# Reordering three stage starts and the last rows of a Griffin layer kernel

## The chip, the cores and the metric

The kernel runs on one core of one Trainium2 chip. A core has TensorE for matmuls (PE in the rows, PEld for the loading of weights, which overlaps), VectorE (DVE), ScalarE (ACT), GpSimd (POOL) and SyncE (SP). SyncE and GpSimd also issue the transfers between the chip's memory (HBM) and the on-chip memory (SBUF). The metric is the device time of one execution in microseconds (us), as a median over runs.

## The reference

One layer of a streaming encoder is computed for 2112 tokens: 2048 of a prompt and 64 of a running stream. In short:

```
h = rmsnorm(x, norm_mix) @ w_in               # split into RG-LRU, attention and gate parts
x1 = x + (lru_part * ... + attention_part) @ w_out
h = rmsnorm(x1, norm_ffn) @ w_up              # 1024 -> 2 * 2816 rows
h = causal_dwconv(h, width 3) + bias          # along time, every row by itself
h = silu(gate rows) * value rows              # 2816 rows
x2 = x1 + h @ w_down                          # 2816 -> 1024
y = rmsnorm(x2, norm_final)
```

The outputs also hold the newest keys, values and states. The change touches nothing in this arithmetic; it concerns the part from `w_up` on.

## The kernel before

**Precision.** Each float32 operand is split into a high part `hi` (a copy in a rounded type, on ScalarE, L205) and a low part `lo = src - hi` (on VectorE, L206); a product is three matmuls, hi·hi, hi·lo and lo·hi. A matmul thus waits for a ScalarE copy and then for a VectorE subtraction. `put2` and `split2` make the copy and hand back the subtraction, to be placed later; three lists hold such subtractions: `plow` (up-projection weights), `dlow` (down-projection operands) and the local list of the token code.

**Tokens.** The 2112 tokens form three pairs of blocks: 304 and 304, 304 and 304, 448 and 448. A pair's tokens of the first and the second block and the halves of the weights form a 2 × 2 block product, done with seven products and sums ahead of and behind them. The products' names in order are 11, T3, T2, T4, T1, 21, 22.

**Up-projection** (profile lines 1066 to 1240, and the loop at 1425). `plan` lists the steps. A step is one product `u` (0 to 6) for two "lanes" of 128 gate or value rows: 24 matmuls (L1105 to L1107). For the first two pairs the two lanes are the two pairs, and weights are read and combined anew (loads L951, combinations L983, stored for later with L971); 22 times 7 steps. Then the third pair follows, 11 times 7 steps, whose lanes are a gate row and a value row block, with the weights stored before (read at L979) and with token operands read back by `xread` (L1050). Behind product u=3, VectorE makes the value rows' first half in a tile G (L1154), behind u=4 the second half (L1156), behind u=5 the gate rows' first half (L1161); ScalarE handles u=0, 1, 2 (L1150) and u=6 (L1163). A PSUM bank is shared by products 0, 2, 4 and 6, so u=6 writes where L1156 reads. Then come the convolution (its first tap on ScalarE, L1135; two more on VectorE for each lane, L1141, four instructions in a row), Silu (L1166), the gating (L1175, L1177), and the sums for the down-projection (L1184 to L1192), stored to `hS`.

**Around it.** `x1prep` prepares the second pair's (index 1) last three operands T1, 21 and 22 while steps 0 to 3 run: it loads the rows of x1, scales them by the norm (L852 on VectorE, L854 and L855 on GpSimd), subtracts (L865), and splits them (L206; L873 and L874 on ScalarE and GpSimd). `norms(2)` makes the third pair's norms (matmul L750, square root L751, reciprocal L752) at step 1 and stores them to `rS`, from which SyncE reads them later (L1008).

**Down-projection** (loop `for j, ... in enumerate(seq)`). `seq` lists product, pair, k (11 blocks of rows), the output row tiles and the columns; an entry is 4 row tiles × 3 matmuls (L1612 to L1614). Weights (`dweights`) and tokens (`dtoken`, read from `hS` at L1272) are split by L206. When k reaches 10, VectorE adds the PSUM results into the sums R (L1652). `drive(side, n)` advances side work by n pieces: at first the rest of the up-projection (`flushing`), later the residual (`resid`, L1564), the squares (`squares`, L1579) and the norm with the output stores (`outputs`, scaling L1592, store L1594). The last product of the first pair ends the program: first two row tiles at 304 columns, then the other two in column halves of 152, each half with its own squares, norm and stores.

**Order.** The program is scheduled by hand: an engine does its instructions in the order in which the code issues them, and only waits for others.

## Time and profile before

| | |
|---|---|
| Median of three runs | 2996.58 us (2990.6 to 2997.52) |
| Profiled run | 2998.43 us, span 2996.7 us |
| Granted TensorE clock, mean | 0.982 |
| TensorE busy | 2874.9 us (96%) |
| VectorE busy | 2059.3 us (69%) |
| ScalarE busy | 1544.9 us (52%) |
| GpSimd busy | 465.2 us (16%) |
| Up-projection | 1578 to 2514 us |
| Down-projection | 2514 to 2987 us, end at 2996.7 |

The profile is of one execution. A timeline row is start, duration, engine, line, operation, output <- input, shape, and the count of like instructions in a row; brackets give the idle time before it and what ended it. A row of the waits gives who waits <- for whom, then total us, times, and the longest. A row of a group gives busy us and mean ns, then idle us before. A window row gives its stretch and length, then for each engine busy us and count, the granted clock (1.00 is full), the DMA share and GB/s.

### The profile page before, as it was taken

To read this page: it belongs to the slowest core of one execution; us is meant where nothing else is said; L and a number is where in the kernel's file an instruction comes from. 1 tells how busy PE (TensorE), PEld (TensorE's weight loads), DVE (VectorE), ACT (ScalarE), POOL (GpSimd) and SP (SyncE) were. 2 spreads that over 40 slices of the span, in tenths; PEclk is the share of its full clock that TensorE was granted. 3 is DMA by queue.
4 is the path that set the end of the run, shared out by engine and by line. 5 is a ranking of instruction groups with operands and counts; after the bars stand their busy time and mean duration, and the time that the engine had idled before them with its cause. 6 is when DMAs were issued, how large, how long until landed. Compare 5 with 4: busy or idle time off the path is not lost. (4 is left out here: it accounts for less than half of the span.)

```text
span 2996.7 us, 48641 instructions
## 1 busy us (share of the span) xinstructions
PE 2874.9 (96%) x17640; PEld 2758.7 (92%) x17640; DVE 2059.3 (69%) x4012; ACT 1544.9 (52%) x3412; POOL 465.2 (16%) x667
## 2 busy tenths in 40 slices
PE   8989999999998999998998999999899999999998
PEld 6989889999998999997997999999799998999997
DVE  5288884277786177776568888888665656666677
ACT  4577772466763367765324555555444444433432
POOL 3232212000000000002324333323111111000011
PEclk9999999999999999999998999999999999999999
DMA  7866547644335734437875565555766666976563
GB/s 239 277 217 204 179 165 229 196 130 133 128 113 186 213 124 139 140 107 259 279 232 181 199 216 207 208 201 198 253 208 218 214 224 193 272 213 211 156 214 118
DMA packets 319185, 583.81 MB, mean 195 GB/s; under 512 B 36464, under 2 KB 221792, under 8 KB 302048
## 3 DMA queue, kind: packets, MB, share of 16 engines
q1 hardware_dynamic: 280544, 449.91, 47.5%
q0 software_dynamic: 38400, 130.79, 11.6%
q8 instruction: 139, 2.28, 0.3%
q14 instruction: 102, 0.84, 0.1%
HBM read 389.46 MB, written 191.64 MB: 194 GB/s over the span
## 5 line engine op out<-in xcount | busy, mean ns | idle before, releaser
L230 PE MATMUL mm<-xh,whl 128*128 128x320 f32 (+2 forms) x2112 | 691.3, 328 | 10.2 <-ACT xh L200 5.5
L231 PE MATMUL mm<-xl,whl 128*128 128x320 f32 (+2 forms) x2112 | 689.0, 326 | 10.2 <-DVE xl L201 5.7
L232 PE MATMUL mm<-xh,whl 128*128 128x320 f32 (+2 forms) x2112 | 687.2, 326 | 1.3 <-POOL whl L201 1.3
L205 ACT ACTIVATE RE<-FW 128x512 fp32r<-128x512 f32 (+2 forms) x540 | 289.0, 559 | 408.3 <-DVE FW L983 101.1
L206 DVE TENSOR_TENSOR RE<-FW,RE 128x512 fp32r<-128x512 f32 (+2 forms) x540 | 315.3, 604 | 173.9 <-ACT RE L205 163.7
L231 PEld LDWEIGHTS mm<-xl,whl 128*128 128x128 f32 x2112 | 402.1, 190 | 18.4 <-DVE xl L201 8.2
L230 PEld LDWEIGHTS mm<-xh,whl 128*128 128x128 f32 x2112 | 402.3, 191 | 17.8 <-ACT xh L200 8.7
L232 PEld LDWEIGHTS mm<-xh,whl 128*128 128x128 f32 x2112 | 402.1, 190 | 2.3 <-POOL whl L201 1.6
L1141 DVE SCALAR_TENSOR_TENSOR FA<-FA,pkt 128x608 f32<-128x608 f32 (+1 forms) x264 | 245.2, 950 | 65.1 <-ACT FA L1135 60.3
L1107 PE MATMUL mf<-RA,RE 128*128 128x304 f32 (+1 forms) x620 | 203.1, 328 | 3.6 <-DVE RE L206 3.6
L1105 PE MATMUL mf<-RA,RE 128*128 128x304 f32 (+1 forms) x620 | 203.3, 328 | 2.0 <-ACT FA L1150 1.7
L1613 PE MATMUL mf<-RE 128*128 128x304 f32 (+2 forms) x616 | 198.1, 322 | 6.6 <-DVE RE L206 6.6
L1106 PE MATMUL mf<-RA,RE 128*128 128x304 f32 (+1 forms) x620 | 202.6, 327 | 0.0
L1612 PE MATMUL mf<-RE 128*128 128x304 f32 (+2 forms) x616 | 198.1, 322 | 2.4 <-DVE RR L1652 2.4
L1614 PE MATMUL mf<-RE 128*128 128x304 f32 (+2 forms) x616 | 197.3, 320 | 0.0
L1106 PE MATMUL mf<-RE 128*128 128x304 f32 (+1 forms) x480 | 158.9, 331 | 15.3 <-DVE RE L206 15.3
L1105 PE MATMUL mf<-RE 128*128 128x304 f32 (+1 forms) x480 | 158.4, 330 | 4.3 <-ACT RE L205 4.3
L1135 ACT ACTIVATE FA<-FA,pkt 128x608 f32<-128x608 f32 (+1 forms) x132 | 128.1, 970 | 63.2 <-DVE FA L1156 61.0
L1107 PE MATMUL mf<-RE 128*128 128x304 f32 (+1 forms) x480 | 158.5, 330 | 0.0
L201 POOL TENSOR_TENSOR gl<-gr,gh 128x256 fp32r<-128x256 f32 x24 | 22.4, 932 | 787.9 <-ACT gh L200 787.9
L510 ACT ACTIVATE pr<-S,nm 128x256 f32<-128x256 f32 (+1 forms) x272 | 123.0, 465 | 12.6 <-DVE nm L506 12.4
L1107 PE MATMUL mm<-RE 128*128 128x304 f32 (+1 forms) x400 | 127.7, 319 | 0.0
(332 smaller groups left out, 7129.1 us busy)
## 6 DMA issues: line engine op xcount, KB each, us to landing
whl<-wiS SPq DMA_DIRECT2D x88, 1024.0 KB, 5.3
wiS<-whl SPq DMA_DIRECT2D x44, 1024.0 KB, 4.8
wuS<-RE POOLq DMA_DIRECT2D x88, 512.0 KB, 4.0
RE<-wuS SPq DMA_DIRECT2D x88, 512.0 KB, 4.3
FW<-in_w_up_dram SPq DMA_DIRECT2D x154, 256.0 KB, 4.4
hS<-FA POOLq DMA_DIRECT2D x154, 152.0 KB, 3.8
FW<-hS SPq DMA_DIRECT2D x154, 152.0 KB, 3.6
FW<-in_w_in_dram SPq DMA_DIRECT2D x44, 512.0 KB, 5.7
```

The lines of the kernel that those rows point to most:

```text
L205: nc.scalar.activation(hi, src, AF.Copy)
L206: return lambda: nc.vector.tensor_tensor(lo, src, hi.bitcast(F32), op=ALU.subtract)
L230: nc.tensor.matmul(ps[:, :n], wh[:, c], xh[:, k, :n], start=first, stop=False)
L231: nc.tensor.matmul(ps[:, :n], wh[:, c], xl[:, k, :n], start=False, stop=False)
L232: nc.tensor.matmul(ps[:, :n], wl[:, c], xh[:, k, :n], start=False, stop=last)
L1105: nc.tensor.matmul(ps[:, :n], w[:, 0, c], x[:, k, 0], start=first, stop=False, **more)
L1106: nc.tensor.matmul(ps[:, :n], w[:, 0, c], x[:, k, 1], start=False, stop=False, **more)
L1107: nc.tensor.matmul(ps[:, :n], w[:, 1, c], x[:, k, 0], start=False, stop=last, **more)
L1141: nc.vector.scalar_tensor_tensor(uc, G[:, j:j + self.cols], col("fw", 44 * j + m), uc, op0=ALU.mult, op1=ALU.add)
L1612: nc.tensor.matmul(ps[m][:, cs], w[:, 0, c], t[:, 0], start=k == 0, stop=False)
L1613: nc.tensor.matmul(ps[m][:, cs], w[:, 0, c], t[:, 1], start=False, stop=False)
L1614: nc.tensor.matmul(ps[m][:, cs], w[:, 1, c], t[:, 0], start=False, stop=k == 10)
```

## The change

1. `x1prep` takes its operands one by one from a list: T1's four pairs first, then 21 and 22. Every scaling is one fused VectorE instruction and every low part is VectorE's; GpSimd's part is gone. Eight buffers are loaded ahead, further loads follow one or two at a time. It is driven by 3, 3, 4 and 0 pieces in steps 0 to 3, the rest in step 3.
2. `norms(2)` and the store of `rS` move from step 1 to step 5.
3. For the third pair, the pool of the gate and value rows G takes its tiles from the other end of its region (`right=True`), and the pending weight low parts `plow` are issued at the start of each step's preparation, whether or not a preparation follows.
4. In the first part of the down-projection, pending low parts `dlow` are issued ahead of the side work.
5. At k = 10 the side work is driven behind the additions, not ahead of them.
6. The last two row tiles run one after the other at 304 columns, in place of two column halves.

```diff
@@ -838,42 +838,34 @@
         for o in ("T1", "21", "22"):
             operand(p, o)
         where = {"11": (0, t0), "12": (0, t1), "21": (4, t0), "22": (4, t1)}
-        x = {}
-
-        def load(k):
-            if k < 4:
-                for o, (half, t) in where.items():
-                    x[o, k] = tp.tile([P, n], F32, name="x" + o, bufs=2)
-                    nc.sync.dma_start(x[o, k], x1S[k + half, :, t:t + n])
-
-        def scale(o, k, eng):
+        todo = [(o, k) for k in range(4) for o in ("12", "11")] + [(o, k) for o in ("21", "22") for k in range(4)]
+        raw, low = [], []
+
+        def load(j):
+            if j < len(todo):
+                half, t = where[todo[j][0]]
+                raw.append(tp.tile([P, n], F32, name="x1", bufs=8))
+                nc.sync.dma_start(raw[j], x1S[todo[j][1] + half, :, t:t + n])
+
+        for j in range(8):
+            load(j)
+        yield
+        for j, (o, k) in enumerate(todo):
             half, t = where[o]
-            if eng is nc.vector:
-                eng.scalar_tensor_tensor(x[o, k], x[o, k], col("g2", k + half), rs[t], op0=ALU.mult, op1=ALU.mult)
-            else:
-                eng.tensor_scalar(x[o, k], x[o, k], col("g2", k + half), None, op0=ALU.mult)
-                eng.tensor_tensor(x[o, k], x[o, k], rs[t], op=ALU.mult)
-
-        load(0)
-        load(1)
-        yield
-        for k in range(4):
-            scale("11", k, nc.vector)
-            scale("12", k, nc.vector)
-            scale("21", k, nc.gpsimd)
-            scale("22", k, nc.vector if k % 2 else nc.gpsimd)
-            nc.vector.tensor_tensor(x["11", k], x["12", k], x["11", k], op=ALU.subtract)
-            yield
-            low = put2(p, "T1", k, x["11", k])
-            yield
-            low()
-            los = []
-            for o in ("21", "22"):
-                t = xops[p, o]
-                nc.scalar.activation(t[:, k, 0], x[o, k], AF.Copy)
-                nc.gpsimd.tensor_tensor(t[:, k, 1], x[o, k], t[:, k, 0].bitcast(F32), op=ALU.subtract)
-            yield
-            load(k + 2)
+            nc.vector.scalar_tensor_tensor(raw[j], raw[j], col("g2", k + half), rs[t], op0=ALU.mult, op1=ALU.mult)
+            while low:
+                low.pop(0)()
+                load(len(raw))
+                if j < 10:
+                    load(len(raw))
+            if o == "12":
+                continue
+            if o == "11":
+                nc.vector.tensor_tensor(raw[j], raw[j - 1], raw[j], op=ALU.subtract)
+                o = "T1"
+            low.append(put2(p, o, k, raw[j]))
+            yield
+        low.pop()()
 
     rsum = {}
     phases = [PAIRS[0], PAIRS[1], PAIRS[2]]
@@ -1277,8 +1269,7 @@
 
     seq = [(i, p, k, range(4), slice(0, PAIRS[p][0][1])) for i in range(7)
            for p in ((2, 0, 1) if i == 0 else (0, 1, 2) if i < 6 else (2, 1)) for k in range(11)]
-    seq += [(6, 0, k, r, c) for r, c in ((range(2), slice(0, BS)), (range(2, 4), slice(0, BS // 2)),
-                                         (range(2, 4), slice(BS // 2, BS))) for k in range(11)]
+    seq += [(6, 0, k, r, slice(0, BS)) for r in (range(2), range(2, 3), range(3, 4)) for k in range(11)]
 
     DRAWS = (10, 13, 16, 19, 22, 24, 26, 28, 30, 32, 34)
 
@@ -1450,7 +1441,7 @@
 
             for pool in up["c"], up["u"], up["h"]:
                 pool.close()
-            up["c"], up["u"], up["h"] = Pool(FA), Pool(FA), Pool(FP)
+            up["c"], up["u"], up["h"] = Pool(FA, right=True), Pool(FA), Pool(FP)
             up["c"].reserve("G", 2 * BM + 2, 3)
             up["u"].reserve("uc", 2 * BM + 2, 4)
         for lane in live:
@@ -1458,6 +1449,8 @@
         if last <= i < last + 7:
             give(0, u)
             give(1, u)
+        while plow:
+            plow.pop(0)()
         while made < len(plan) + 1 and fits(i):
             prepare(made)
             made += 1
@@ -1467,21 +1460,21 @@
             lane.after(u)
         rounded()
         if i < 4:
-            drive(x1, 3)
+            drive(x1, (3, 3, 4, 0)[i])
             if i == 0:
                 io[2].close()
                 wr.extend("wr", 4 * P, 2)
-            if i == 1:
-                norms(2)
-                for t0, n in PAIRS[2]:
-                    nc.gpsimd.dma_start(rS[:, t0:t0 + n], rsum[t0])
             if i == 3:
                 drive(x1, 99)
                 x1.clear()
                 tp.close()
                 sums[1].close()
-                sums[2].close()
                 up["u"].reserve("uc", 2 * BS, 4)
+        if i == 5:
+            norms(2)
+            for t0, n in PAIRS[2]:
+                nc.gpsimd.dma_start(rS[:, t0:t0 + n], rsum[t0])
+            sums[2].close()
         if i == 6:
             up["s"].close()
             up["s"], up["h"] = Pool(FW), Pool(FA, right=True)
@@ -1626,7 +1619,12 @@
                 tparts(len(seq) - 36 + k)
             if k < 6:
                 raw[6, 0, k - 2] = dtoken("T4", 0, k - 2)
-        drive(side, 5 if R is None else 1 if i < 4 else 2 if (i, p) != (6, 0) or j < len(seq) - 22 else 3)
+        pace = 5 if R is None else 1 if i < 4 else 2 if (i, p) != (6, 0) or j < len(seq) - 22 else 3
+        if R is None:
+            while dlow:
+                dlow.pop(0)()
+        if k < 10:
+            drive(side, pace)
         if j == 8:
 
             drive(side, 99)
@@ -1666,6 +1664,7 @@
                 add("11", "11")
             if i == 6:
                 add("21", "21")
+        drive(side, pace)
         if i == 2:
             side.append(resid(p, "11"))
         if i == 3:
```

In the order of VectorE's instructions, the change shows at these places. Line numbers of the changed kernel are lower by 8 around the up-projection (L1148 is L1156 of before, L1133 is L1141, L975 is L983, L864 is L865); L855 is the new scaling, in place of L852.

VectorE in the up-projection's steps 1 to 3 before, from two scalings and a subtraction of pair 1's operands on (FA holds these, FW weights and norms, RE split operands):

```order
L852 SCALAR_TENSOR_TENSOR FA<-FA,pkt,FW 128x304 x3
L865 TENSOR_TENSOR FA<-FA 128x304
L752 RECIPROCAL FW<-FW 128x448 x2
L206 TENSOR_TENSOR RE<-FW,RE 128x512
L983 TENSOR_TENSOR FW<-FW 128x512
L206 TENSOR_TENSOR RE<-FA,RE 128x304
L852 SCALAR_TENSOR_TENSOR FA<-FA,pkt,FW 128x304 x2
L865 TENSOR_TENSOR FA<-FA 128x304
L206 TENSOR_TENSOR RE<-FW,RE 128x512
L1154 TENSOR_TENSOR FA<-mf,FA 128x304
L1154 TENSOR_TENSOR FA<-mm,FA 128x304
L206 TENSOR_TENSOR RE<-FA,RE 128x304
```

VectorE in steps 3 to 5 of the changed kernel:

```order
L855 SCALAR_TENSOR_TENSOR FA<-FA,pkt,FW 128x304
L206 TENSOR_TENSOR RE<-FA,RE 128x304
L855 SCALAR_TENSOR_TENSOR FA<-FA,pkt,FW 128x304
L206 TENSOR_TENSOR RE<-FA,RE 128x304 x2
L206 TENSOR_TENSOR RE<-FW,RE 128x512
L975 TENSOR_TENSOR FW<-FW 128x512
L1148 TENSOR_TENSOR FA<-mf,FA 128x304 x2
L206 TENSOR_TENSOR RE<-FW,RE 128x512
L975 TENSOR_TENSOR FW<-FW 128x512
L1133 SCALAR_TENSOR_TENSOR FA<-FA,pkt 128x608 x4
L1153 TENSOR_TENSOR FA<-mm,FA 128x304 x2
L752 RECIPROCAL FW<-FW 128x448 x2
```

The two reciprocals L752 stood between the operands of k = 1 and k = 2, ahead of step 3's evictions L1154; they now stand behind step 5's evictions L1153, and operand by operand a scaling is followed by a low part.

VectorE at the down-projection's start before (FP and FW hold tokens and weights, RE the split parts; the 448-wide L206 are tokens):

```order
L206 TENSOR_TENSOR RE<-FW,RE 128x512 x2
L1141 SCALAR_TENSOR_TENSOR FA<-FA,pkt 128x898 x4
L206 TENSOR_TENSOR RE<-FW,RE 128x448 x4
L206 TENSOR_TENSOR RE<-FW,RE 128x512
L1175 TENSOR_TENSOR FP<-FA 128x832
L1177 TENSOR_TENSOR FP<-FA 128x64
```

The same place in the changed kernel:

```order
L206 TENSOR_TENSOR RE<-FW,RE 128x512 x2
L206 TENSOR_TENSOR RE<-FW,RE 128x448 x4
L206 TENSOR_TENSOR RE<-FW,RE 128x512
L1133 SCALAR_TENSOR_TENSOR FA<-FA,pkt 128x898 x4
L206 TENSOR_TENSOR RE<-FW,RE 128x448
L206 TENSOR_TENSOR RE<-FW,RE 128x512
```

The four token low parts and a weight's stood behind the convolution L1141 and stand ahead of it now (L1133).

VectorE at the end of the program before, from the scalings of the pair's other block on (RR holds the sums, FD the squares and norms):

```order
L1592 SCALAR_TENSOR_TENSOR RR<-RR,pkt,FD 128x304 x8
L1579 TENSOR_TENSOR FD<-FD 128x304 x2
L1652 TENSOR_TENSOR RR<-mf,RR 128x152 x2
L1579 TENSOR_TENSOR FD<-FD 128x152 x2
L752 RECIPROCAL FD<-FD 128x152
L1592 SCALAR_TENSOR_TENSOR RR<-RR,pkt,FD 128x152 x8
L1652 TENSOR_TENSOR RR<-mf,RR 128x152 x2
L1579 TENSOR_TENSOR FD<-FD 128x152 x2
L752 RECIPROCAL FD<-FD 128x152
L1592 SCALAR_TENSOR_TENSOR RR<-RR,pkt,FD 128x152 x8
```

The same place in the changed kernel (L1585 is L1592, L1572 is L1579, L1650 is L1652):

```order
L1585 SCALAR_TENSOR_TENSOR RR<-RR,pkt,FD 128x304 x8
L1572 TENSOR_TENSOR FD<-FD 128x304 x2
L1650 TENSOR_TENSOR RR<-mf,RR 128x304
L1572 TENSOR_TENSOR FD<-FD 128x304
L1650 TENSOR_TENSOR RR<-mf,RR 128x304
L1572 TENSOR_TENSOR FD<-FD 128x304
L752 RECIPROCAL FD<-FD 128x304
L1585 SCALAR_TENSOR_TENSOR RR<-RR,pkt,FD 128x304 x8
```

Two sets of additions, squares, reciprocal and eight scalings at 152 columns become one set at 304, with the row tiles' additions apart.

## The prediction

> **What bounds the kernel now.** I read the busy times first, then who TensorE (PE) waits for in the second half of the program, then the busy times stage by stage, then the timelines at the places found.
>
> ```profile
> span 2996.7 us, 48641 instructions
> PE 2874.9 (96%) x17640; PEld 2758.7 (92%) x17640; DVE 2059.3 (69%) x4012; ACT 1544.9 (52%) x3412; POOL 465.2 (16%) x667
> PE mf L1106 <- DVE RE L206: 15.3, 5, 5.2
> PE mf L1613 <- DVE RE L206: 6.6, 1, 6.6
> 1578.48:1621.18 42.70, 30.11 (x174) 27.44 (x172) 37.96 (x47) 16.00 (x37) 26.14 (x29) 0.80 0.52 179
> 2113.14:2167.07 53.93, 41.26 (x170) 36.07 (x169) 33.74 (x58) 23.14 (x53) 5.34 (x10) 0.87 0.75 262
> 2514.28:2550.95 36.67, 30.07 (x133) 26.90 (x132) 22.21 (x37) 18.44 (x39) 4.31 (x8) 0.86 0.76 234
> 1630.00:1640.00 10.00, 10.00 (x73) 10.00 (x73) 6.03 (x13) 4.43 (x11) 0.68 (x2) 1.00 0.60 205
> 2200.00:2210.00 10.00, 10.00 (x50) 9.09 (x49) 5.94 (x7) 7.22 (x20) 0.00 (x0) 1.00 0.50 157
> ```
>
> Columns of the stage rows: length, busy time of PE, of its weight loads, of VectorE (DVE), ScalarE (ACT) and GpSimd (POOL), granted clock, DMA share, GB/s. PE is the bound: 96% of the span, and 10.00 of 10 us inside a stage. There a 304-wide matmul costs 10/73 = 0.137 us and a 448-wide one 10/49 = 0.204 (by the weight loads), so a step of 24 costs 3.3 and 4.9. What the change can win lies where PE stops: three stage starts, of 42.70, 53.93 and 36.67 us, at a granted clock of 0.80 to 0.87. In all three the missing operand is a low part (L206 on VectorE). The edit touches them, the additions that close a down-projection pass, and the end.
>
> **A. Start of the up-projection (pair-1 operands, norms).**
>
> ```profile
> 1578.48 0.30 PE L1105 MATMUL mf<-RA,RE 128*128 128x304 f32 x1
> 1601.82 0.62 PE L1106 MATMUL mf<-RE 128*128 128x304 f32 x1 [4.11 <-DVE RE L206]
> 1621.18 0.30 PE L1105 MATMUL mf<-RA,RE 128*128 128x304 f32 x1
> 1584.86 1.15 DVE L852 SCALAR_TENSOR_TENSOR FA<-FA,pkt,FW 128x304 f32<-128x304 f32 x2
> 1588.79 4.12 DVE L852 SCALAR_TENSOR_TENSOR FA<-FA,pkt,FW 128x304 f32<-128x304 f32 x3
> 1594.34 5.76 DVE L752 RECIPROCAL FW<-FW 128x448 f32<-128x448 f32 x2 [1.04 <-ACT FW L751]
> 1613.07 0.85 DVE L1156 TENSOR_TENSOR FA<-mf,FA 128x304 f32<-128x304 f32 x2
> L852 DVE SCALAR_TENSOR_TENSOR FA<-FA,pkt,FW 128x304 f32<-128x304 f32 x10 | 8.5, 896 | 0.0
> L206 DVE TENSOR_TENSOR RE<-FW,RE 128x512 fp32r<-128x512 f32 x10 | 8.5, 857 | 2.5 <-ACT RE L205 2.4
> 2974.53 3.66 DVE L1592 SCALAR_TENSOR_TENSOR RR<-RR,pkt,FD 128x304 f32<-128x304 f32 x8
> 2538.07 2.36 DVE L206 TENSOR_TENSOR RE<-FW,RE 128x448 fp32r<-128x448 f32 x4
> ```
>
> Steps 0 to 6 run from 1578.48 to 1621.18; their 168 matmuls are worth 168 × 0.137 = 23.0. The difference, 19.7, less 1.5 for the norms' own matmuls, is the most that A can win: about 18. In between VectorE is busy 37.96 of 42.70, in the order the rows show: operands of pair 1, the two reciprocals of the third pair (5.76, with 1.04 of waiting ahead), more operands, and only at 1613.07 the evictions L1156 that free the bank into which step 6 writes.
>
> The edit removes GpSimd's twenty tensor instructions, and gives VectorE 16 scalings (10 before), 4 subtractions and 12 low parts (4 before): 14 more 304-wide instructions. It takes the reciprocals behind step 5's evictions. Priced as where VectorE works alone: a scaling 3.66/8 = 0.46; another 304-wide one 0.85/2 = 0.42; a 448-wide low part is 2.36/4 = 0.59, so a 512-wide one about 0.65. Ahead of the end of L1156 there now stand 16 scalings (7.3), 20 other 304-wide ones (4 subtractions, 12 low parts, 4 evictions: 8.5) and 7 of 512 (4.5), in all 20.3. From the first, at 1584.9, they end at 1605.2, where they ended at 1613.9. Each is there in time before that: T1 needs 16 instructions (some 7.9, 1592.8, with step 4 at about 1593), operand 21 twelve more.
>
> So step 6 begins at 1605.2 and step 7 at about 1608.5 to 1609, against 1621.18. What is late next is the reciprocals: they begin behind the first four L1141 and L1161, at about 1609.4, last 5.76, and two weight low parts follow, to 1616.5; step 9 needs these at 1609 + 2 × 3.3 = 1615.7 and waits 0.8. The net gain I take is **11.4**. Nothing on the DMA side moves: the same 16 loads, in 8 buffers one behind the other; the 20 ScalarE copies are the same.
>
> The unknown is the contended price. In this stage ten scalings cost 0.896 each and ten 512-wide low parts 0.857, beside a GpSimd busy for 26.14 us; alone they cost 0.46 and 0.65. At the high price throughout, 16 × 0.896 + 20 × 0.80 + 7 × 0.857 = 36.3, L1156 would end at 1621, and step 6, which began at 1621.18 − 3.3 = 1617.9, would begin 3.3 later: a loss. I take the low price because GpSimd's tensor work, the only thing on that engine that is longer than an issue, is gone. Bounds −3.3 and +14.
>
> The Trainium skill, page "SBUF — State Buffer", section "Who interferes with whom", says that a VectorE instruction with two inputs in SBUF contends with a GpSimd instruction that reads SBUF, the first one there blocking the other whole. The 4.12 us for three scalings beside 0.46 each alone look like that. By the page A is worth the 11.4; if the slow rows have another cause it is worth less, down to the lower bound.
>
> **B. Third pair's gate rows at the other end; weight low parts flushed each step.**
>
> ```profile
> 2117.36 0.47 PE L1107 MATMUL mf<-RA,RE 128*128 128x448 f32 x1 [3.65 <-DVE RE L206]
> 2149.56 0.73 PE L1106 MATMUL mf<-RE 128*128 128x448 f32 x1 [5.24 <-DVE RE L206]
> 2148.35 0.62 DVE L1154 TENSOR_TENSOR FA<-mf,FW 128x448 f32<-128x448 f32 x1 [4.67 <-DMA hS<-FA]
> 2160.89 0.74 PE L1106 MATMUL mf<-RE 128*128 128x448 f32 x1 [3.41 <-DVE RE L206]
> 2154.64 4.60 DVE L1141 SCALAR_TENSOR_TENSOR FA<-FA,pkt 128x898 f32<-128x898 f32 x4
> 2151.43 1.81 ACT L205 ACTIVATE RE<-FP 128x448 fp32r<-128x448 f32 x3 [5.08 <-DMA FP<-xS]
> RE<-wuS SPq DMA_DIRECT2D x14, 512.0 KB, 7.0
> ```
>
> The first two waits (3.65 and 5.24) go: the low parts that PE waited for at 2117.36 now stand ahead of the conv (L1141) on VectorE, and L1154 no longer waits 4.67 for a store (hS from FA) to free old rows, behind which three low parts were queued. But PE's next needs do not move with it. The kept weights of the second step are loads of 512 KB that take 7.0 here and are issued as before; a PE that is 3.65 earlier waits for them. The operand needed at 2160.89 stands behind four L1141 (4.60), these behind ScalarE, and ScalarE behind a load that ended its 5.08 us of waiting at 2151.43; nothing of that chain waits for what is removed. So PE again stops until about 2160.9, and I take **0**. Bounds: −1 (a conv that now waits for stores), and 9, were both waits won in full.
>
> A new idle stretch of some 5 us at the second step would leave PE at a low clock for some us; it lies ahead of the same 2160.89. The Trainium skill ("TensorE: Matmul & The Clock Gate", "HAM oscillation — how this bites in real kernels") puts the loss of clock at idle gaps above about 3.4 us. By the page the 3.65 us gap may cost clock as much as the new one, so B's sum stays at 0.
>
> **C. Start of the down-projection (token low parts ahead of the last conv).**
>
> ```profile
> 2526.20 0.74 PE L1613 MATMUL mf<-RE 128*128 128x448 f32 x1 [6.60 <-DVE RE L206]
> 2521.01 4.60 DVE L1141 SCALAR_TENSOR_TENSOR FA<-FA,pkt 128x898 f32<-128x898 f32 x4 [4.09 <-ACT FA L1135]
> 2525.53 2.82 DVE L206 TENSOR_TENSOR RE<-FW,RE 128x448 fp32r<-128x448 f32 x5
> 2536.46 0.63 DVE L1188 TENSOR_TENSOR FP<-FP 128x448 f32<-128x448 f32 x1 [3.93 <-DMA hS<-FP]
> ```
>
> The first pass is 132 matmuls of 448, worth 132 × 0.204 = 26.9, and took 36.67: 9.7 too long, of which 6.60 is one wait. VectorE stood idle 4.09 for ScalarE ahead of the conv, and the low parts stood behind it. They need only their high halves and now run in that idle time, done before 2520; PE loses neither the 6.60 nor the some 2 us of low clock behind it. What is late next: the conv ends no later than about 2526, as its releaser is the same, but the later token low parts still stand behind L1188, which waits for a store until 2536.46. PE, 8.7 ahead, then stops at the ninth block of rows for 1.5 to 2.4. I take **7**; bounds 4 (that store and its successors hold PE longer) and 8.7.
>
> **D. Additions ahead of the side work.**
>
> ```profile
> 2844.50 0.41 PE L1612 MATMUL mf<-RE 128*128 128x304 f32 x1 [0.78 <-DVE RR L1652]
> 2883.84 0.47 PE L1612 MATMUL mf<-RE 128*128 128x448 f32 x1 [1.61 <-DVE RR L1652]
> ```
>
> Both waits stood behind two scalings L1592 (0.46 each, 0.9 together), which now come behind the additions: 0.78 + 0.9 = **1.7**; bounds 0.5 and 2.4. At the other closings PE waited for nothing, and that side work loses its place by some 2 us only.
>
> **E. Last rows in full width.**
>
> ```profile
> 2980.89:2986.95 6.06, 6.06 (x56) 6.06 (x55) 3.60 (x10) 0.39 (x1) 0.00 (x0) 1.00 0.34 102
> L1612 PE MATMUL mf<-RE 128*128 128x152 f32 x44 | 12.3, 280 | 0.0
> 2972.44 2.05 DVE L752 RECIPROCAL FD<-FD 128x304 f32<-128x304 f32 x1 [0.65 <-ACT FD L751]
> 2989.33 1.10 DVE L752 RECIPROCAL FD<-FD 128x152 f32<-128x152 f32 x1 [1.04 <-ACT FD L751]
> 2990.47 2.39 DVE L1592 SCALAR_TENSOR_TENSOR RR<-RR,pkt,FD 128x152 f32<-128x152 f32 x8
> 2990.87 3.65 SPq L1594 DMA_DIRECT2D out_yT_dram<-RR  x8
> ```
>
> A 152-wide matmul costs 6.06/55 = 0.11. The 132 of them (44 on each of three lines) are worth 14.6; 66 of 304 are 9.0: 5.6 less, and one set of the norm's matmuls inside PE's order is gone, some 1 more. So the last matmul ends at about 2980.2, not 2986.95. Against that the last chain grows, since all 304 columns now come last: from the last matmul to the reciprocal 2.4 before, about 3.1 with wider instructions (2983.3), reciprocal 2.05 (1.10 before) to 2985.4, a first scaling of 0.46, then eight issues in 3.65 as now, to 2989.5, and as much behind the last issue as now (2996.7 − 2994.5 = 2.2) and 0.3 for twice the bytes: 2992.0. Gain **4.7**; bounds 3 and 5.8.
>
> **Sum.** 11.4 + 0 + 7 + 1.7 + 4.7 = 24.8: span 2971.9. The profiled run took 2998.43, 1.73 more than its span and 1.85 more than the median 2996.58; so 2973.6 for a profiled run and **2972** as the median. The likeliest case's own range, its bounds not all hit at once, is 2965 to 2982.
>
> **Rivals.**
> 1. *B pays in full.* For: the two waits of 3.65 and 5.24 are the largest left there, and an earlier PE frees weight buffers earlier, so loads may be issued earlier. Against: the load behind ScalarE's 5.08. It gives 5 to 9 more, about 2965.
> 2. *The contended prices stay.* If writes of transfers and not GpSimd made VectorE slow (DMA share 0.52 there), A is −3.3 and the whole 10.1: 2986.5.
> 3. *The waits only move.* The change then doesn't do what it says: C's store and A's ScalarE copies leave only a third of their 18.4, some 6; with D and E's 6.4 that is 12.4: 2984, and 2990 if D and E are hidden too.
> 4. *Slower: the late norms stop SyncE's queue.* The reader of the third pair's norms stands in SyncE's queue ahead of weight loads; their store now comes at about 1618 instead of 1603, and every load behind the read waits with it. Weights behind it are needed at about 1633, so 15 us of slack. It decides only if the reciprocals slip past 1633; each us more is a us of PE, and 24.8 are eaten at 1658; at 1665 the time would be about 3004.
>
> **How the numbers follow.** Chances: forecast 0.62, rival 1 0.17, rival 2 0.08, rival 3 0.08, rival 4 0.05. The range 2962 to 2985 holds the forecast's own and rival 1 and the edge of 3. About 9 us (0.3%) is what a measurement here tells from none, so faster is below 2987.6: the forecast, rival 1, and half each of rivals 2 and 3, which lie at that edge: 0.87; same 0.08, their other halves; slower 0.05.
>
> **What would show it.** Right, if step 7 begins near 1609 with scalings of 0.46 to 0.53 in between, if PE still stops before about 2161, if the 6.60 at the down-projection is gone with a smaller wait near its ninth block, if no PE wait for L1652 above 0.8 is left, and if the last matmul stands some 12 us ahead of the end. Wrong, if VectorE's scalings stay near 0.9, if PE runs through the third pair's start, or if SyncE's loads stand still around 1618.

## The result and the profile after

The changed kernel took 2978.22 us as a median (2973.40 to 2983.68), the kernel before 2995.52 on the same chip: 17.3 us less, ratio 0.9941 with a 95% interval of 0.9923 to 0.9959. The forecast was 2972, range 2962 to 2985. A second, longer measurement (in the experiments) gave 2970.69 against 2995.72, 25.0 less, ratio 0.9925 (0.9905 to 0.9944).

The page of the changed kernel, and then whom TensorE waits for from 1550 us on (total, times, longest):

```profile
span 2981.9 us, 48462 instructions
PE 2863.3 (96%) x17572; PEld 2746.4 (92%) x17572; DVE 2054.1 (69%) x4013; ACT 1545.0 (52%) x3409; POOL 445.1 (15%) x647
```

```profile
PE mf L1098 <- DVE RE L206: 7.0, 3, 6.7
PE mf L1097 <- DMA RE<-wuS: 5.8, 1, 5.8
PE mf L1097 <- ACT FA L1142: 4.1, 3, 1.8
PE mf L1097 <- ACT FW L1142: 3.8, 3, 1.5
PE mf L1606 <- DVE RE L206: 3.5, 1, 3.5
PE mf L1605 <- DVE RR L1650: 0.7, 1, 0.7
```

Three rows of the same view of the kernel before, beside the 15.3 and 6.6 of the prediction:

```profile
PE mf L1107 <- DVE RE L206: 3.6, 1, 3.6
PE mf L1105 <- ACT FA L1150: 1.7, 1, 1.7
PE mf L1105 <- ACT FW L1150: 0.3, 1, 0.3
```

The 18.9 us of waiting for VectorE's low parts in the up-projection (15.3 and 3.6; L1106 and L1107 before, L1098 now) have become 7.0, the 6.6 at the down-projection 3.5, and the 2.4 for additions 0.7. Kept weights are a new name (wuS, 5.8), and the waits for ScalarE's evictions (L1150 before, L1142 now) have grown from 2.0 to 7.9. The three stage starts, in the same columns as before:

```profile
1577.11:1609.33 32.22, 27.55 (x173) 25.72 (x172) 29.84 (x60) 16.71 (x38) 4.31 (x8) 0.95 0.68 226
2105.97:2160.55 54.58, 40.23 (x170) 34.94 (x169) 33.60 (x57) 23.45 (x54) 5.34 (x10) 0.87 0.72 261
2507.75:2540.19 32.44, 28.96 (x134) 26.02 (x132) 22.48 (x37) 18.14 (x39) 4.31 (x8) 0.95 0.76 233
```

From the start times of TensorE's matmuls the span divides as follows (us; "again" is the second profile of the changed kernel, from the run e_same):

| stretch | before | changed | gain | forecast gain | again |
|---|---|---|---|---|---|
| up to the first matmul of the up-projection | 1578.5 | 1577.1 | 1.4 | 0 | 1577.8 |
| up-projection, steps 0 to 6 | 42.7 | 32.2 | 10.5 | 12.2 | 29.7 |
| steps 7 to 10 | 13.4 | 18.1 | −4.7 | −0.8 | 18.1 |
| the other steps of the first two pairs | 478.6 | 478.6 | 0 | 0 | 478.6 |
| third pair, first seven steps (B) | 53.9 | 54.6 | −0.6 | 0 | 53.9 |
| third pair, the rest | 347.2 | 347.2 | 0 | 0 | 340.5 |
| down-projection, first pass (C) | 36.7 | 32.4 | 4.2 | 7.0 | 31.9 |
| from there to the last matmul (D, part of E) | 436.2 | 430.0 | 6.2 | 8.5 | 427.8 |
| end (rest of E) | 9.5 | 11.7 | −2.2 | −2.1 | 11.7 |
| span | 2996.7 | 2981.9 | 14.7 | 24.8 | 2969.9 |

**A.** The first row is the scalings of pair 1, then come the two kinds of low parts, all within the stretch 1578.48 to 1621.18 of the changed kernel; behind them, where TensorE stops next (timeline rows of TensorE, ScalarE and VectorE):

```profile
L855 DVE SCALAR_TENSOR_TENSOR FA<-FA,pkt,FW 128x304 f32<-128x304 f32 x16 | 8.4, 528 | 0.0
L206 DVE TENSOR_TENSOR RE<-FW,RE 128x512 fp32r<-128x512 f32 x10 | 6.6, 679 | 0.8 <-ACT RE L205 0.7
L206 DVE TENSOR_TENSOR RE<-FA,RE 128x304 fp32r<-128x304 f32 x12 | 5.6, 469 | 0.4
```

```profile
1611.61 5.75 DVE L752 RECIPROCAL FW<-FW 128x448 f32<-128x448 f32 x2
1617.18 0.42 ACT L1142 ACTIVATE FW<-mf 128x304 f32<-128x304 f32 x1 [3.67 <-DMA rS<-FW]
1617.66 0.41 PE L1097 MATMUL mf<-RA,RE 128*128 128x304 f32 x1 [1.47 <-ACT FW L1142]
1623.95 0.41 PE L1097 MATMUL mf<-RA,RE 128*128 128x304 f32 x1 [1.50 <-ACT FW L1142]
```

Scalings cost 528 ns where they cost 896, the 512-wide low parts 679 (857 before). Behind the reciprocals ScalarE's eviction waits 3.67 us for the store of rS, because its target tile lies in the room that the norms' tiles have just left, and that store still reads them.

**B and C.** The last two long waits of TensorE in the third pair and what stands in front of the second; then the wait in the first pass of the down-projection:

```profile
2116.76 0.74 PE L1097 MATMUL mf<-RA,RE 128*128 128x448 f32 x1 [5.77 <-DMA RE<-wuS]
2148.63 4.60 DVE L1133 SCALAR_TENSOR_TENSOR FA<-FA,pkt 128x898 f32<-128x898 f32 x4
2154.88 0.74 PE L1098 MATMUL mf<-RE 128*128 128x448 f32 x1 [6.65 <-DVE RE L206]
2529.15 0.62 DVE L1180 TENSOR_TENSOR FP<-FP 128x448 f32<-128x448 f32 x1 [4.04 <-DMA hS<-FP]
2531.43 0.65 PE L1606 MATMUL mf<-RE 128*128 128x448 f32 x1 [3.48 <-DVE RE L206]
```

**E.** The end: reciprocal, scalings and stores, each now once, at 304 columns:

```profile
2973.18 2.05 DVE L752 RECIPROCAL FD<-FD 128x304 f32<-128x304 f32 x1 [1.42 <-ACT FD L751]
2975.27 3.65 DVE L1585 SCALAR_TENSOR_TENSOR RR<-RR,pkt,FD 128x304 f32<-128x304 f32 x8
2975.83 3.77 SPq L1587 DMA_DIRECT2D out_yT_dram<-RR  x8
```

### The profile page after: what moved, and what is told of

Its sections match the earlier page's. It is cut to its first block, busy times and chain, and to the rows that moved or that the text cites. A ratio compares the mean times of both kernels' runs of the same rounds, so it can differ in the third digit from the quotient of the medians.

```text
span 2981.9 us, 48462 instructions
## 1 busy us (share of the span) xinstructions
PE 2863.3 (96%) x17572; PEld 2746.4 (92%) x17572; DVE 2054.1 (69%) x4013; ACT 1545.0 (52%) x3409; POOL 445.1 (15%) x647
## 3 DMA queue, kind: packets, MB, share of 16 engines
q0 software_dynamic: 38400, 130.79, 11.7%
## 5 line engine op out<-in xcount | busy, mean ns | idle before, releaser
L205 ACT ACTIVATE RE<-FW 128x512 fp32r<-128x512 f32 (+2 forms) x540 | 288.7, 559 | 405.0 <-DVE FW L975 97.3
L206 DVE TENSOR_TENSOR RE<-FW,RE 128x512 fp32r<-128x512 f32 (+2 forms) x540 | 313.6, 601 | 168.9 <-ACT RE L205 162.8
L231 PEld LDWEIGHTS mm<-xl,whl 128*128 128x128 f32 x2112 | 401.7, 190 | 17.3 <-DVE xl L201 7.4
L1133 DVE SCALAR_TENSOR_TENSOR FA<-FA,pkt 128x608 f32<-128x608 f32 (+1 forms) x264 | 245.3, 950 | 60.3 <-ACT FA L1127 55.5
L1098 PE MATMUL mf<-RA,RE 128*128 128x304 f32 (+1 forms) x616 | 201.3, 327 | 0.0
L1606 PE MATMUL mf<-RE 128*128 128x304 f32 (+1 forms) x594 | 192.3, 324 | 3.5 <-DVE RE L206 3.5
L1605 PE MATMUL mf<-RE 128*128 128x304 f32 (+1 forms) x594 | 192.5, 324 | 0.7 <-DVE RR L1650 0.7
L1607 PE MATMUL mf<-RE 128*128 128x304 f32 (+1 forms) x594 | 191.4, 322 | 0.0
L1098 PE MATMUL mf<-RE 128*128 128x304 f32 (+1 forms) x476 | 156.1, 328 | 7.0 <-DVE RE L206 7.0
L1097 PE MATMUL mf<-RE 128*128 128x304 f32 (+1 forms) x476 | 156.0, 328 | 2.4 <-ACT RE L205 1.5
L1099 PE MATMUL mf<-RE 128*128 128x304 f32 (+1 forms) x476 | 156.0, 328 | 0.0
L1097 PEld LDWEIGHTS mf<-RA,RE 128*128 128x128 f32 x616 | 116.6, 189 | 18.6 <-DMA RE<-wuS 6.1
```

The costliest lines, as they stand in the source:

```text
L205: nc.scalar.activation(hi, src, AF.Copy)
L206: return lambda: nc.vector.tensor_tensor(lo, src, hi.bitcast(F32), op=ALU.subtract)
L231: nc.tensor.matmul(ps[:, :n], wh[:, c], xl[:, k, :n], start=False, stop=False)
L1097: nc.tensor.matmul(ps[:, :n], w[:, 0, c], x[:, k, 0], start=first, stop=False, **more)
L1098: nc.tensor.matmul(ps[:, :n], w[:, 0, c], x[:, k, 1], start=False, stop=False, **more)
L1099: nc.tensor.matmul(ps[:, :n], w[:, 1, c], x[:, k, 0], start=False, stop=last, **more)
```

## The experiments

All but the last are edits of the changed kernel, judged by their profiles against its own; the code shown is the pieces that matter. Where an edit does not touch them, the stretches above repeat to about a microsecond, except for three things that differ from run to run whatever the edit: where VectorE's first scaling of pair 1 falls (5.5 to 9.6 us behind the first matmul of the up-projection, which moves everything behind it), the rate of the 448-wide matmuls, and how much of a stop is followed by a low granted clock (both in the last section). So times are counted from the first scaling: 23.7 us from there to step 7 in the changed kernel, 36.3 in the kernel before. In the runs that leave this order alone step 7 comes at 23.7 where step 6 runs at a granted clock of 1.00 (3.5 us), and at 25.2 or 25.3 where it runs at 0.66 (5.0 us). There steps 7 to 10 are shorter by as much (16.8 and 16.9 us), because the stop ahead of step 9 shrinks: step 11 comes at 41.4 to 42.2 in all of them, and the third pair at 520.0 to 520.8. In the kernel before these are 49.7 and 528.3.

**GpSimd beside VectorE.** Was it GpSimd that made the scalings slow? Twenty idle multiplications, or twenty fills, were put among the operands of `x1prep`:

```diff
+            for _ in range(2 if j % 4 == 0 else 1):   # ga, gb: two tiles of their own
+                nc.gpsimd.tensor_tensor(ga, ga, gb, op=ALU.mult)   # second run: nc.gpsimd.memset(ga, 0.0)
             nc.vector.scalar_tensor_tensor(raw[j], raw[j], col("g2", k + half), rs[t], op0=ALU.mult, op1=ALU.mult)
```

> The changed kernel with 20 extra GpSimd multiplications of 128x304 (two inputs in SBUF, in tiles nobody else uses) between the operands of the second pair; they compute nothing that is used. Theory 'GpSimd': a VectorE instruction with two inputs is slowed by a GpSimd instruction that reads, so the mean of the sixteen scalings L855 goes from about 0.53 us towards the 0.90 of before while GpSimd works, and the eviction L1148 and with it step 7 come 3 to 9 us later. Rival 'transfers': the slow rows of before came from the transfers written meanwhile; the scalings stay at 0.53 to 0.6, and step 7 within 1 us.

> As the run with extra GpSimd multiplications, but with 20 GpSimd fills (memset of 128x304), which write and read nothing. If only GpSimd's reads stand against VectorE's second input, the scalings stay at about 0.53 us and step 7 within 1 us of the changed kernel's 32.2; if any GpSimd work slows VectorE, they rise as in the other run.

Groups in the run with the multiplications, and pieces of its timeline:

```profile
L861 DVE SCALAR_TENSOR_TENSOR FA<-FA,pkt,FW 128x304 f32<-128x304 f32 x16 | 15.1, 948 | 0.0
L860 POOL TENSOR_TENSOR FA<-FA 128x304 f32<-128x304 f32 x20 | 19.2, 960 | 1.5
```

```profile
1592.82 12.54 POOL L860 TENSOR_TENSOR FA<-FA 128x304 f32<-128x304 f32 x12
1604.59 1.11 DVE L206 TENSOR_TENSOR RE<-FA,RE 128x304 fp32r<-128x304 f32 x1
1605.62 0.52 DVE L861 SCALAR_TENSOR_TENSOR FA<-FA,pkt,FW 128x304 f32<-128x304 f32 x1
1606.07 0.46 DVE L206 TENSOR_TENSOR RE<-FA,RE 128x304 fp32r<-128x304 f32 x1
```

The same groups in the run with the fills:

```profile
L861 DVE SCALAR_TENSOR_TENSOR FA<-FA,pkt,FW 128x304 f32<-128x304 f32 x16 | 8.4, 530 | 0.0
L860 POOL MEMSET FA<- 128x304 f32 x20 | 7.1, 355 | 1.0
```

In the run with multiplications a scaling costs 948 ns in the mean, in the run with fills 530. Instruction by instruction: the ten scalings under a multiplication took 1.09 to 1.65 us and the six clear of one 0.52 to 0.53, while the six that ran almost wholly under a fill took 0.53, as the other ten did. The price falls from 1.11 to 0.46 us at the very instruction at which GpSimd's run of twelve ends (1592.82 + 12.54 = 1605.36). From the first scaling, step 7 begins at 36.8 us with the multiplications, and at 25.3 with the fills. Shown: GpSimd's reading instructions make VectorE slow, and taking them away is what A won in steps 0 to 6, beside the norms' move (e_early, below, divides the two). In the kernel before they cost 3.7 us on ten scalings (896 against 528 ns) and 1.8 on ten 512-wide low parts (857 against 679), and with the 304-wide instructions some 8. The Trainium skill ("SBUF — State Buffer", "Who interferes with whom") has it that a VectorE instruction with two SBUF inputs contends with a GpSimd one that reads SBUF, and not with one that only writes; both halves of that agree with the 948 and the 530.

**The late norms, three ways.** What gave back 4.7 us in steps 7 to 10: the room of the norms' tiles, or the reciprocals themselves?

```diff
 # e_room: the tiles' room is handed back behind the new lanes' tiles
             lane_sums(BS)
+            sums[2].close()                # before: at step 5
 # e_early: norms(2) and the store of rS at step 1, all else as changed
 # e_late: one norm each at steps 12 and 15, their reader (fill) from step 18
+        if i in (12, 15):
+            t0, n = PAIRS[2][i == 15]
+            rms(rsum[t0], n, rsum[t0])
```

> The changed kernel, with the room of the third pair's norm tiles handed back after the first lanes' sum tiles p1, p7 and V have been placed at step 6, not before. Theory 'room': steps 8 to 10 stand still because ScalarE's evictions (L1142) write into the tiles that the late store of rS still reads (3.67 and 2.41 us of waiting on that store). Then these waits go, and step 11 begins about 45.6 to 46.5 us after the first matmul of the up-projection, against 50.3 in the changed kernel: 4 to 4.7 us less. Rival 'VectorE': the weight low parts behind the two reciprocals are late anyway (the prediction's 0.8 us); then PE waits for L206 at step 9 and most of the 4.7 stays.

> The changed kernel with the third pair's norms back at step 1. Theory: the rS store is early again and the waits of ScalarE at steps 8 to 10 go (4.7 us), but 5.76 us of reciprocals and a wait of about 1 stand ahead of the operands and of L1148 again, so step 7 begins 4 to 7 us later than the 32.2 us after the first matmul that it has in the changed kernel; step 11 begins within 3 us of the 50.3 of the changed kernel. Rival: VectorE has slack there, step 7 stays within 1.5 us of 32.2, and step 11 comes at about 46.

> The changed kernel with the third pair's two norms at steps 12 and 15 in place of step 5 (one each), and the reader of those norms started at step 18 instead of 7. Theory 'reciprocals': the 4.7 us given back between step 7 and step 11 are the price of 5.76 us of reciprocals on VectorE where PE runs right behind it, whichever wait names them; with both gone from there, steps 7 to 11 take 13.4 us (four steps at the full rate) against 18.1 in the changed kernel, and the reciprocals cost nothing at steps 12 to 18, where VectorE has some 40% of its time free: the first two pairs' stage is 4 to 5 us shorter. Rival: the same bubble comes back where the reciprocals go, and the stage stays within 1 us.

The run e_room: TensorE's first stop after step 7, the Silu that waits for the convolution on VectorE, and the stop behind it:

```profile
1621.22 0.41 PE L1099 MATMUL mf<-RA,RE 128*128 128x304 f32 x1 [1.49 <-DVE RE L206]
1625.75 0.71 ACT L1158 ACTIVATE FA<-FA 128x608 f32<-128x608 f32 x1 [0.70 <-DVE FA L1133]
1626.83 0.41 PE L1097 MATMUL mf<-RA,RE 128*128 128x304 f32 x1 [2.27 <-ACT FW L1142]
```

Steps 7 to 10 took 17.7 us there, against 16.6 to 18.1 in the runs with the room as changed and 13.4 at the full rate. ScalarE no longer waits for the store, yet TensorE stands still as long: once for the weight low part behind the reciprocals, and once for an eviction that stands on ScalarE behind the Silu, which waits for the convolution, which stands behind the same reciprocals. So the theory of the room falls as the cause; the store is one of two equally long ways from the reciprocals to TensorE. With the norms early, steps 7 to 10 take 13.4, but TensorE waits 5.6 us for the evictions ahead of step 6 and step 7 comes 32.1 behind the first scaling, 8.4 later:

```profile
PE mf L1097 <- DVE FA L1148: 5.6, 1, 5.6
```

Moving the norms from step 1 to step 5 was thus worth 8.4 − 4.7 = 3.7, and the third pair says the same (524.1 us behind the first scaling, against 520.4). This run also divides A's gain: of the 12.6 us by which step 7 came nearer to the first scaling (36.3 to 23.7), 4.2 are there with the norms still at step 1 (32.1), so they are the operands' new preparation, without GpSimd; 8.4 are the norms' move, of which 4.7 are lost again by step 11.

With the norms late, steps 7 to 10 take 13.4 too, and from step 7 to the third pair it is 493.7 us against 496.6: of the 4.7, 2.9 remain, since 1.8 come back in steps 12 to 20, where the norms' own matmuls are no longer hidden by a stop. But in this run step 6 took 6.1 us at a granted clock of 0.52, and with no stop behind it to take that up, step 7 came 26.3 us behind the first scaling. So from the first scaling to the third pair it is 520.1 against 520.4, a gain of 0.3; in e_all and e_all_nob, below, where step 6 ran at 0.66, it is 519.0, a gain of 1.4. The norms' own matmuls had filled 1.5 us of the stop ahead of step 6; without them TensorE waits 3.6 there in e_late and 2.1 in e_all_nob, where it waits 2.1 or 0.6 with them, and a longer stop is likelier to cost clock (last section). Moving the norms to steps 12 and 15 was thus worth 0.3 to 1.4 here; the 2.9 would need a step 6 at full clock, which none of the three runs had.

**The third pair.** Without the change (e_undo_b), and with the token operands' low parts also issued ahead of the convolutions (e_xlow):

```diff
 # e_undo_b
-            up["c"], up["u"], up["h"] = Pool(FA, right=True), Pool(FA), Pool(FP)
+            up["c"], up["u"], up["h"] = Pool(FA), Pool(FA), Pool(FP)
-        while plow:
-            plow.pop(0)()
 # e_xlow: xread keeps its pending low part in a list xlow
         while plow:
             plow.pop(0)()
+        while xlow:
+            xlow.pop(0)()
```

> The changed kernel without the third pair's change (gate rows at the old end of the region, weight low parts flushed only with a preparation). Theory 'worth nothing': PE's wait of 5.77 us for kept weights and of 6.65 us for an operand turn into the old 3.65, 5.24 and 3.41, and the third pair's first seven steps take the same 53.5 to 55 us. Rival 'worth its two waits': they take 5 us or more longer.

> The changed kernel with the low part of the newest token operand of the third pair issued at the start of a step, ahead of the convolutions, like the weights' low parts. Theory 'SyncE': the kept weights come late because SyncE waits some 6 us for an operand's buffer, whose low part stands on VectorE behind four convolution instructions (3.3 us) and two evictions; with it ahead of them, SyncE goes on some 3.5 us earlier, PE's first wait falls from 5.8 to about 2, and the last one, 6.65 behind four 898-wide convolutions, to about 3: the third pair's first seven steps take 46 to 51 us against 53.5 to 54.6. Rival 'bandwidth': the transfers are at 0.9 to 1.0 of their engines there and land as late as before; 53 or more.

TensorE's waits at the third pair's start without the change (two rows), and with the low parts first (two rows):

```profile
PE mf L1098 <- DVE RE L206: 8.3, 2, 5.1
PE mf L1099 <- DVE RE L206: 2.8, 1, 2.8
```

```profile
PE mf L1099 <- DVE RE L206: 4.4, 2, 3.9
PE mf L1098 <- DMA RE<-wuS: 0.4, 1, 0.4
```

Undone, the seven steps take 52.9 us; with the change they took 53.1 to 54.6 in eight profiles. B is worth nothing, or costs up to 1.6 (one profile without it). With the low parts first they take 48.8: 4 to 6 less. Where the difference comes from is in SyncE's waits, in the changed kernel and in e_xlow:

```profile
SPq L1042 <- DVE RA L206: 9.0, 3, 6.2
```

```profile
SPq L1041 <- DVE RA L206: 10.9, 6, 2.4
```

The longest wait of SyncE for an operand's buffer falls from 6.2 to 2.4; the kept weights queued behind it are issued that much earlier, and TensorE's 5.8 for them becomes 0.4 (SyncE's waits together are no fewer, 9.0 and 10.9 us, and TensorE now waits 3.3 for ScalarE's copies). The rival, that the transfers are at their limit, falls.

**The first pass of the down-projection.** Smaller pieces of side work, so that the ninth block's token low part stands ahead of the subtraction that waits for a store:

```diff
-        pace = 5 if R is None else 1 if i < 4 else ...
+        pace = (5 if j < 2 else 2) if R is None else 1 if i < 4 else ...
```

> The changed kernel with the side work at the down-projection's start in pieces of 2 from the third block on (5 before), so that the low part of the ninth block's tokens stands ahead of the subtraction L1180 that waits for a store. Theory: PE's wait of 3.5 us at the ninth block and the low clock behind it go; what is left is the next low part behind the same store, 0.5 to 1.5 us; the first pass takes 28 to 30 us against 32.0 to 32.8. Rival: the side work that comes later holds the next blocks as long, and the pass stays at 32.

```profile
PE mf L1606 <- DVE RE L206: 1.5, 1, 1.5
```

The pass took 28.5 us, against 31.9 to 32.8 in eight profiles that keep the changed order here. The ninth block ran without a stop (2.4 us); the tenth stopped for 1.5 behind the same store. The forecast's remaining stall had the right place, and this removes most of it. Two runs do not fit that size, and both have the gate rows at the old end: e_undo_b, without the smaller pieces, took 30.1, as its stop of 2.65 us at the ninth block was followed by no low clock (5.35 us for the block, against 7.74 at a clock of 0.78 in the changed kernel); and e_all_nob, below, with them, took 30.7, as its stop of 2.33 at the tenth was followed by one (6.4 us at 0.73). With the gate rows there, a gain of the smaller pieces is not shown.

**Together, and the changed kernel again.** Five rounds each, on one chip: the changed kernel unaltered (e_same), with the edits e_late, e_xlow and e_cpace together (e_all), and with these but the gate rows at the old end (e_all_nob).

> The changed kernel once more, unaltered, on the chip of the following two runs. By the first measurement 17 us faster than before (0.994 of it); by the sum of its own stages, with the first stage and the rate of the 448-wide matmuls taken out as chance, 14 to 16 us (0.995). Its profile again shows the step 5 to 11 pattern (18 us for steps 7 to 11), 53 to 54.6 us for the third pair's first seven steps and 32 to 32.8 for the first pass of the down-projection.

> The changed kernel with the three edits together: norms at steps 12 and 15, the newest token low part ahead of the convolutions, side work in pieces of 2. By their profiles they are worth 3 (4.7 less 1.7 of norm matmuls and small waits at steps 13 to 21), 5 and 4 us, at places that do not touch: 12 us less than the changed kernel, 0.990 to 0.991 of the kernel before. Rival: a later stage takes it back (the weight loads are at their limit behind the third pair's start), and it is 6 or less.

> As the run with the three edits, but the third pair's gate rows at the old end of the region. If the first wait was SyncE's and the region's end only decided who was named at the second one, the third pair's first seven steps take the same 48 to 50 us and the time is the same within 3 us. Rival: with the first wait gone the store of the old rows (4.67 us of waiting on VectorE in the kernel before) comes onto the path, and the stage is 3 to 5 us longer.

| | median us | ratio to before | 95% interval |
|---|---|---|---|
| before | 2995.72 | | |
| e_same | 2970.69 | 0.9925 | 0.9905 to 0.9944 |
| e_all | 2965.66 | 0.9904 | 0.9889 to 0.9919 |
| e_all_nob | 2963.28 | 0.9899 | 0.9881 to 0.9917 |

In the profile of e_all the third pair's first seven steps take 49.1 us (53.9 in e_same) and the first pass 28.7 (31.9): these two edits repeat their own worth. The late norms do not: steps 7 to 10 take 13.4 (18.1), but the slow step 6 and the norms' own matmuls leave 1.4 of it. End to end it is 5.0 less than e_same, 7.4 for e_all_nob, where 12 were expected, and the intervals overlap: for e_all the rival's size, 6 or less, is what came. Of what is missing, 1.6 is the norms' part (3 were counted). From the first pass to the last matmul e_all took 430.8, e_same 427.8; three waits for ScalarE's copies (L205, 1.9 us in all) are new there, the rest was not traced. The gate rows' end (48.7 against 49.1 us for the seven steps) makes no difference at the third pair's start: the rival of the old rows' store falls.

**The kernel before, once more.**

> The kernel before, unaltered, profiled once more. In the profiles so far a 448-wide matmul of the third pair's stage takes either 0.2025 or 0.207 us from one start to the next, for whole stages (1848 of them: 7 to 8 us), whatever the edit, and both kernels of the comparison showed 0.207. Theory 'chance': the rate is drawn at the restart after a stop of TensorE; a second profile of the kernel before may show either, and its stages A, C and the end repeat within 3 us (A 42.7 for steps 0 to 6, less what the first scaling comes later or earlier; third pair's first seven steps 52 to 55; first pass 36.7). Rival: the kernel before always has 0.207 and part of the gain of the changed kernel is a faster rate.

Its span was 2997.0; steps 0 to 6 took 42.6 us, the third pair's first seven steps 52.5, the first pass 36.1, the end 9.5. The reference of the table above is sound. Its 448-wide matmuls were slow in the third pair's later steps once more, so whether it ever draws the fast rate there stays open.

## Why the prediction was right or wrong

- **A, steps 0 to 6: right.** The sum of 20.3 us of VectorE instructions, at the price without GpSimd, put step 6 at 20.3 us behind the first scaling and step 7 at 24; they came at 20.3 and 23.7. The choice between the bounds was the decisive one, and the two GpSimd runs show that it was made for the right reason. The 0.896 of the forecast is a mean duration and its 0.46 a spacing of instructions that overlap, so the like of 0.896 is 0.53, and the lower bound was drawn somewhat too low. That step 6 ran at full clock in this profile was luck: in three others of the same order for it (the fills, the multiplications and the smaller pieces) it ran at 0.66 and took 1.5 us more. The first scaling fell 2.1 us later than in the profile of before, which lies within its spread.
- **A, "what is late next is the reciprocals … waits 0.8": the step that failed.** The place was right, the size was not: 4.7 us. To step 11 A thus won 7.9 us from the first scaling (49.7 to 41.8), where 11.4 were forecast. I followed only the weight low parts. The convolution, the Silu behind it and ScalarE's evictions behind that stand in the same line, and so does the store of rS with the tiles in its room. 5.76 us put on VectorE (busy for 16.97 of the 18.07 us of steps 7 to 10), with TensorE one step behind, cost 4.7 of them.
- **B, 0: right, with its mechanism.** The wait went to the kept weights (5.77) and to the operand behind the four convolutions (6.65). What I did not see is what held the kept weights: not the size of the loads but SyncE standing 6.2 us for one buffer. The bound of 9 for "both waits won" was therefore no fantasy: 4 to 6 of it were to be had by another low part.
- **C, 7: mis-sized, 4.2.** The 6.60 went, and the new stall came at the ninth block behind L1180's wait for a store, as written. It was a stop of 3.48 and 1.8 of low clock behind it (the block took 7.74 us for 2.48), not 1.5 to 2.4: the low part stood behind two further subtractions as well, and I had counted no clock.
- **D, 1.7: right.** From 2.39 to 0.7.
- **E, 4.7: 4.4.** From the norm's first matmul near the end to the last matmul it is 9.5 us, 16.1 before: 6.6 less, as forecast (5.6 and 1; 132 times 0.11 is 14.5, not 14.6, which changes nothing). The end grew by 2.2 (2.1 forecast). The 6.2 between the first pass and the last matmul are smaller than D and E's 8.3 because of a new stop of 1.5 for ScalarE's copy (L205) at 2586.05, and some tenths elsewhere; e_same does not show that loss (427.8).
- **Rivals.** *B pays in full*: no. *Contended prices stay*: no, by the two GpSimd runs. *The waits only move*: true of B, of 4.7 us in A and of 5.3 in C. *SyncE's queue stands for the late norms*: it did stand for rS (its read was issued only at 1617.13, and the next weight load behind it at 1623.04), but no wait of TensorE for those loads followed: this rival's mechanism was there, and its price was nothing.
- **The time.** The span fell by 14.7 in the first profile and by 26.8 in the second, of the same program. Of the 12.0 between them 6.7 lie in the third pair's later steps, where nothing but the rate of a matmul differs, 2.6 in where the first scaling falls, and 2.2 behind the down-projection's first pass. That the median came 6 above the forecast in the first measurement and 1 below it in the second is therefore partly luck: A and C fell short by 3.5 and 2.8 (B by 0.6 more), and the faster rate, which the forecast had not counted, gave back 6.7.

## What to carry to other kernels

An instruction moved out of an engine's way is paid where it lands: follow every engine that waits behind it there, down to who frees the next buffer and room, and not only the first wait that comes to mind. Where TensorE waits for a low part, look at what the issuing queue of its weights waits for, since one early entry that waits for a buffer holds all transfers behind it. Before work is shared out to GpSimd, compare the price of VectorE's two-input instructions with and without it: here twenty GpSimd instructions cost VectorE some 8 us and spared it 14 instructions of 0.46. And price an edit over a stretch that ends where the runs agree again: steps 7 to 10 alone said 4.7 for the late norms, the stretch up to the third pair 0.3 to 1.4.

## What the runs showed of the hardware

A 448-wide matmul with its own weight load has two rates at a granted clock of 1.00, and keeps one through all the later steps of the third pair. Windows of 100 us there, in the changed kernel's two profiles:

```profile
2200.00:2300.00 100.00, 100.00 (x485) 90.83 (x485) 59.67 (x88) 41.94 (x102) 11.33 (x21) 1.00 0.63 214
```

```profile
2200.00:2300.00 100.00, 100.00 (x495) 92.69 (x494) 60.05 (x89) 43.49 (x112) 11.30 (x21) 1.00 0.65 219
```

485 against 494 weight loads in 100 us: 0.206 and 0.202 us each, 347.2 and 340.5 us for the stretch of the table, and the same program drew either. It is not drawn at a stop alone: in the third pair's first steps of e_early the rate went from 206.7 ns to 202.7 and back between 2125 and 2133 us, at a granted clock of 1.00 and without a stop. In the stretch of the table the fast rate stood in nine of the twelve profiles of changed kernels (both rates on one chip) and in neither of the two of the kernel before; what decides it is open, and so is whether a part of the 17 to 25 us is owed to it. In the first two pairs the 304-wide matmuls showed one rate only. It may also be why ten timings of the changed kernel spread from 2967.8 to 2983.7.

The granted clock has two values here, 1.00 and 0.50, and changes only on a fixed grid of 3.41 us. In each of the 14 traces the stretches at 0.50 begin whole multiples of 3.41 apart and last one to five of them (the last is cut by the end of the span). What goes before a change is how busy TensorE was in the grid's window ahead of it. Windows of that grid, two by two: at the stop ahead of step 6, 2.12 us in e_same and in e_cpace alike, and at the stop in the down-projection's first pass, 2.65 us in e_undo_b and 2.33 in e_all_nob:

```profile
1599.63:1603.04 3.41, 2.24 (x10) 1.14 (x8) 3.24 (x8) 1.33 (x3) 0.00 (x0) 1.00 0.54 214
1603.04:1606.46 3.42, 2.47 (x17) 2.48 (x18) 3.37 (x6) 2.77 (x8) 0.53 (x1) 1.00 0.02 8
```

```profile
1602.86:1606.27 3.41, 1.34 (x4) 0.38 (x2) 3.24 (x8) 1.08 (x3) 0.00 (x0) 1.00 0.32 130
1606.27:1609.68 3.41, 3.36 (x13) 3.36 (x14) 3.33 (x6) 3.38 (x10) 0.53 (x1) 0.50 0.28 113
```

```profile
2529.45:2532.86 3.41, 2.44 (x12) 1.88 (x10) 0.61 (x2) 1.29 (x3) 0.00 (x0) 1.00 1.01 325
2532.86:2536.27 3.41, 1.73 (x9) 1.61 (x10) 3.41 (x8) 0.55 (x2) 1.61 (x3) 1.00 1.07 324
```

```profile
2509.43:2512.84 3.41, 1.45 (x8) 1.00 (x6) 1.91 (x4) 1.58 (x5) 0.99 (x2) 1.00 0.41 138
2512.84:2516.25 3.41, 3.03 (x8) 2.73 (x9) 3.41 (x8) 0.00 (x0) 0.62 (x2) 0.50 0.90 254
```

A window with TensorE busy for 1.34 or 1.45 us is followed by one at 0.50, those with 1.73 or more are not (behind 2536.27 the clock stays at 1.00). From 1500 us on, in the 14 traces together, TensorE was busy for less than 0.45 of a full-clock window 74 times, and each time the next window ran at 0.50; above 0.57 that never happened, and in between it went both ways (10 times and 25). So one and the same stop of 2.12 us cost clock or not by where it fell on the grid, and the length alone, which the prediction took at some 3.4 us, does not decide. No edit tested this rule.
